# Bias tables of a neighbourhood attention: assembled in DRAM ahead of time, loaded with one transfer each

## The chip, the cores and the metric

The kernel runs on one core of one Trainium2 chip. The metric is device time in microseconds of one execution, and the median of several runs is compared. The core has five engines with a queue each, executed in order: TensorE (PE, with its weight loads as PEld), VectorE (DVE), ScalarE (ACT), GpSimd (POOL) and SyncE (SP). SP computes nothing; in this kernel it issues nearly all DMA transfers. Sixteen DMA engines carry them out. PEclk is the clock that the throttle granted to PE, as a share of full speed.

## The reference

One layer of a diffusion backbone over 1024 latent tokens (a grid of 16 rows by 64 columns) and 256 context tokens, model width 1024: a modulated RMSNorm, one input projection to attention heads and to a Hyena long-convolution group, both groups side by side, an output projection, and a SwiGLU feed-forward part. What the change touches is the learned bias of the neighbourhood attention. There are 8 heads of 64; each query sees a window of 8 rows by 16 columns and all context keys, in one softmax:

```python
dr = row_idx - r[:, None] + (WIN_ROWS - 1)
dc = jnp.clip(col[None, :] - col[:, None], -(WIN_COLS - 1), WIN_COLS - 1) + (WIN_COLS - 1)
bias = rpb[:, dr[:, None, :, None], dc[None, :, None, :]].astype(jnp.float32)
s_loc = jnp.einsum('bhrqd,bhrikd->bhrqik', qg, k_band).astype(jnp.float32) * scale
s_loc = jnp.where(col_in[None, None, None, :, None, :], s_loc + bias[None], NEG)
...
p = jax.nn.softmax(jnp.concatenate([s_loc, s_ctx], axis=-1), axis=-1).astype(v.dtype)
```

`rpb` has 15 row offsets by 31 column offsets for each head; `NEG` is -1e30, so that places outside the window weigh nothing.

## The kernel before

A planner puts the instructions of each engine in order: it takes the program's order as priority, estimates when each can start, and inserts the semaphores. A tile with one buffer (`bufs=1`) passes from one user to the next in program order, and the next user waits until the former is done with it. What an engine's queue holds is fixed at build time; if an instruction's input is late, everything behind it on that engine waits too.

The stages that matter, with their times in the profile:

- **Projection** (to about 606 us). A loop over j = 0 to 3 and `which` = 0 to 2 calls `qkv(j, which)` and `hy_chunk(which, j)`. Each calls `proj`, which loads 128 columns of weights (L606, tile `wr`), splits them into a high and a low part and does 72 matmuls per 128 columns (L116 to L118) into three PSUM banks of tag `p`. A `sink` evicts the banks: `qkv` to a tile `cv0` or `cv1`, `hyin` likewise with a width-3 convolution (L638 to L646). These two `cv` tiles take turns. `hy_chunk` then makes sums and differences in the tile `fo` (L663 to L667, one buffer), transposes them and stores them to `lxd` and `cxd`. Pieces of the modulation (`adaln`, tile `wada` with one buffer, L221 and L225) are put between.
- **Filters.** Inside the first turn, `filters` builds the spectra of the Hyena filters, with PE work of its own (L376, and L116 to L118 into banks `fA` and `fB`). The planner mixes it with the projection until about 420 us.
- **Bias frames.** After the turn j = 0, `rpb_frames` runs for three variants (`var`: left edge, middle, right edge of the grid). Each fills a tile with `NEG` on POOL, places the 16 windows of columns with 16 small loads (L556), reorders it (L557) and stores it to the DRAM tensor `rpw` as variant x query column x head x 4 x 120 (L558). These frames use the tile `fo`.
- **Chains.** `chain(j)`, j = 0 to 4, does the long convolution by matmuls with DFT tables and twiddles, on PE (L802, L872), DVE (L816 to L860), POOL (L823 to L885) and ACT; it loads `s` (L788) and `K` (L837) on SP and stores `hyd`. Chains have a raised priority; they start beside the projection and go on beside the attention.
- **Attention** (606 to about 917 us). `attend(p_)` works on a pair of heads. It loads q, k and v (L1004 to L1010) and the bias tables `tbs[h][var]`: six tiles of 128 x 736 f32, one per head of the pair and variant, with one buffer each. A table holds 128 queries (8 rows by 16 columns), for the upper and the lower half of the grid side by side (11 and 12 key rows by 32 columns). All of it outside the windows is `NEG`, filled once by POOL before the loop (L941). `bias_load` writes the rest: for each of 16 query rows one copy (L959) from `rpw`, because the window moves with the row. That makes 16 copies a table of 64 pieces of 256 B, 96 a pair, 384 in all. `scores` multiplies q by k (L1021), and one DVE instruction (L1042) adds the table to the scores and takes the row maximum; exponentials on ACT (L1055, L1056), transposes (L1065), the product with v (L979) and the normalisation (L1111) follow.
- **Output projection and feed-forward** (after 917 us): not touched.

Of the kernel before, what the change touches and what calls it, by code (L numbers as in the profile page):

```python
# [11 lines left out]
F32 = mybir.dt.float32  # L12
# [7 lines left out]
P = 128  # L20
# [3 lines left out]
LT = LL + LC  # L24
NH, DH = 8, 64
# [4 lines left out]
NEG = -1e30  # L30
# [44 lines left out]
HALF_ROWS = ((0, 11), (4, 12))  # L75
# [11 lines left out]
def _build(nc, tc, top, V, A, G, T, Q, I, O, dbg, upto):  # L87
# [458 lines left out]
    NROW = HALF_ROWS[0][1] + HALF_ROWS[1][1]  # L546
    HOFF = (0, HALF_ROWS[0][1] * 32)
    rpw = dr.tile([3, 16, NH, 4, 120], F32, name="rpw")

    def rpb_frames(t, var):  # L550
        f, g = t[:, 0:480], t[:, 512:992]
        G.memset(f, NEG)
        fv = f.rearrange("p (r c) -> p r c", c=32)
        for cq in range(16):
            a = (8 + max(cq - 8, 0), cq, min(cq, 8))[var]
            Q.dma_start(out=fv[cq * 8:cq * 8 + 8, :, a:a + 16], in_=I["rpb"][0][:, :, a + 7 - cq:a + 23 - cq])  # L556
        G.tensor_copy(g.rearrange("p (u r c) -> p r u c", u=4, r=15), f.rearrange("p (r u c) -> p r u c", u=4, r=15))  # L557
        Q.dma_start(out=rpw[var].rearrange("q h u x -> (q h) (u x)"), in_=g)  # L558
# [93 lines left out]
    def hy_chunk(which, j):  # L652

        cv = hyin((8, 0, 4)[which] + j)
        v = cv[:, 0:LL].rearrange("p (j r) -> p r j", r=4)
        lo, up = v[:, :, 0:128], v[:, :, 255:127:-1]
        clo, cup = cv[:, LL:LL + 128], cv[:, LL + 255:LL + 127:-1]
        fo = ip.tile([P, 2, 640], F32, tag="fo", name="fo", bufs=1)
        for i in range(2):
            d, dc = fo[:, i, 0:512].rearrange("p (r j) -> p r j", r=4), fo[:, i, 512:640]  # L660
            if which < 2:
                f = G.tensor_sub if i else G.tensor_add
                f(d, up, lo)  # L663
                f(dc, cup, clo)
            else:
                A.copy(d, up if i else lo)
                V.tensor_copy(dc, cup if i else clo)  # L667
        for i in range(2):
            ps = bk("tB")
            for r in range(4):  # L670
                T.transpose(ps[:, r * P:(r + 1) * P], fo[:, i, r * P:(r + 1) * P], ident)
            t = ip.tile([P, 512], F32, tag="st", name="st", bufs=2)
            A.copy(t, ps)
            Q.dma_start(out=lxd[j, which, :, i], in_=t)
        ps = bk("tB")
        for i in range(2):
            T.transpose(ps[:, i * P:(i + 1) * P], fo[:, i, 512:640], ident)
        t = ip.tile([P, 2, P], F32, tag="st", name="cx", bufs=2)
        A.copy(t, ps[:, 0:256].rearrange("p (i c) -> p i c", i=2))
        Q.dma_start(out=cxd[which, :, :, j * P:(j + 1) * P], in_=t)  # L680

    def qkv(p_, which):


        w_ = 16 if which == 0 else 8
        t = ip.tile([P, LT], F32, tag=f"cv{turn_('cv')}", name="qkv", bufs=1)

        def sink(ps, c0, n):
            if c0 < LL:
                r0 = c0 // GW  # L690
                src = ps.rearrange("p (r u c) -> p r u c", r=n // GW, c=w_)
                A.copy(t[:, 0:LL].rearrange("p (u r c) -> p r u c", r=16, c=w_)[:, r0:r0 + n // GW], src)
            else:
                A.copy(t[:, LL:LT], ps)

        proj(win[:, :, which * 512 + p_ * P:which * 512 + (p_ + 1) * P], sink, DH ** -0.5 if which == 0 else 1.0)
        if which < 2:
            Q.dma_start(out=(qd, kd)[which][p_, :, 0:LT], in_=t)
        if which == 0:
            return  # L700
        ctx = t[:, LL:LT]
        ps = bk("tB")
        for i in range(2):
            T.transpose(ps[:, i * P:(i + 1) * P], ctx[:, i * P:(i + 1) * P], ident)
        pv = ps[:, 0:256].rearrange("p (n c) -> p n c", n=2)
        so = ip.tile([P, 2, P], F32, tag="st", name="so", bufs=2)
        A.copy(so, pv)
        for i in range(2):
            Q.dma_start(out=O[1 + which][0, 0, 2 * p_:2 * p_ + 2, i * P:(i + 1) * P].rearrange("h t d -> t h d"),
                        in_=so[:, i].rearrange("p (h d) -> p h d", h=2))  # L710
        if which == 2:
            vstore(so, 8, 2, p_)
            for g in range(2):
                ps = bk("tB")
                for i in range(4):
                    T.transpose(ps[:, i * P:(i + 1) * P], t[:, (4 * g + i) * P:(4 * g + i + 1) * P], ident)
                vt = ip.tile([P, 4, P], F32, tag="st", name="vt", bufs=2)
                A.copy(vt, ps.rearrange("p (n c) -> p n c", n=4))
                vstore(vt, 4 * g, 4, p_)
# [17 lines left out]
    for j in range(4):  # L737
        for which in range(3):
            if j + which > 0:
                qkv(j, which)  # L740
            hy_chunk(which, j)
            if j + which == 0:

                t = ft([P, 512], "tm", bufs=2)
                e = "p a b -> p (a b)"
                Q.dma_start(out=t, in_=I["t_dft"].flatten().rearrange("(p x) -> p x", p=P))
                split(t, dft[0].rearrange(e), dft[1].rearrange(e))
                Q.dma_start(out=dlt, in_=I["t_delta"])
                Q.dma_start(out=nt, in_=I["t_nt"])
                with tc.issue_after(wloads[-1]):  # L750
                    Ws0 = w3load(0)
                filters(hs1, hs2, Ws0)
        cached(j)
        if j == 0:
            for var in range(3):
                rpb_frames(ip.tile([P, LT], F32, tag="fo", name="rp", bufs=1), var)
    fes.close()
    fbk.close()
    cbk = Banks("bkc", "right", "tile", cA=(1, 3))
# [176 lines left out]
        V.memset(t, 0.0)  # L936

    tbs = [[tp.tile([P, NROW * 32], F32, name=f"tb{h}{v}") for v in range(3)] for h in range(2)]
    for t in tbs:
        for v in t:  # L940
            G.memset(v, NEG)  # L941

    BLK = ((1, 4), (0, 4), (0, 4), (0, 3))
    Pring = [[tp.tile([P, 2, b - a, 16, 8], F32, name=f"Pl{h}{i}") for i, (a, b) in enumerate(BLK)] for h in range(2)]
    for r in Pring:
        for t in r:
            G.memset(t[:, 0, :, 11:16], 0.0)
            G.memset(t[:, 1, :, 0:4], 0.0)
    def bias_load(h, var):

        t = tbs[h % 2][var]
        for half in range(2):
            for rq in range(8):
                r = 8 * half + rq
                r0 = min(max(r - 4, 0), 8)
                nr = HALF_ROWS[half][1]
                a, d = r0 - HALF_ROWS[half][0], r0 - r + 7
                tv = t[rq * 16:(rq + 1) * 16, HOFF[half]:HOFF[half] + nr * 32].rearrange("q (u x) -> q u x", u=4)
                Q.dma_start(out=tv[:, :, a * 8:a * 8 + 64], in_=rpw[var, :, h, :, d * 8:d * 8 + 64])  # L959

    def stat(name, n=2):
        return tp.tile([P, n], F32, tag=name, name=name, bufs=4)

# [37 lines left out]
    def attend(p_):  # L1001
# [9 lines left out]
                        in_=I["cache_ctx_v"][0, 0, 2 * p_ + h].rearrange("(n p) d -> p n d", p=P))  # L1011
        for var in range(3):
            for h in range(2):
                bias_load(2 * p_ + h, var)
        kg = k[:, 0:LL].rearrange("p (u x) -> p u x", u=8)
        hs = [slice(h * DH, (h + 1) * DH) for h in range(2)]
        Pc = {}
# [747 lines left out]
```

## Time and profile before

| | us |
|---|---|
| three runs: lowest, median, highest | 1920.3, 1921.23, 1921.35 |
| the profiled execution: its time | 1918.35 |
| its span, from first to last instruction | 1916.6 |

Over the span PE is busy 1748.7 us (91%), DVE 1372.6 us (72%), ACT 885.0 us (46%) and POOL 412.4 us (22%); the mean granted clock of PE is 0.947. These are averages over stages that differ much: in the first slices of the feed-forward part all of PE's time is taken, while in the slices of the attention it is 0.7 to 0.9. So what follows is read by stretches of time, one row a stretch: start and end, its length, the busy time of PE, PEld, DVE, ACT and POOL, each with its number of instructions, then the granted clock, the share of the 16 DMA engines that was busy, and GB/s. In rows of the timeline the first number is the start, the second the duration; brackets hold the idle time before it and what ended it. A row of waits reads: who waited for whom, us in total, times, the longest one. A row of an instruction group in a tile's view has the shortest, median and longest duration in ns.

The transfer counts by kind show how much SP has to issue for the tables: `tb<-rpw` x384 of 16.0 KB each; the next most frequent kinds are `wada<-in_w_ada_dram` and `rp<-in_rpb_dram` with x48 each.

### The profile page before, as it was taken

What the parts mean: (1) busy time and instruction counts of PE and PEld (TensorE: products, weight loads), DVE (VectorE), ACT (ScalarE), POOL (GpSimd) and SP (SyncE); (2) the same over time, 40 slices, a digit from 0 to 9 for tenths busy, and PEclk for the clock granted to TensorE, in tenths of its full rate; (3) what the DMA queues carried; (4) which work ended last, traced back from release to release, by engine and by line L of the source; (5) the groups of instructions that cost most, each with busy time, mean ns of one, the idle gap of its engine ahead of it and who ended that gap; (6) DMA issues with size and microseconds to landing.
All of it is one profiled execution on the core that took longest, in us unless ns stands there. A gap on an engine that the chain in (4) does not pass through costs nothing.

```text
span 1916.6 us, 27816 instructions
## 1 busy us (share of the span) xinstructions
PE 1748.7 (91%) x9999; PEld 1468.5 (77%) x9999; DVE 1372.6 (72%) x2175; ACT 885.0 (46%) x1827; POOL 412.4 (22%) x331
## 2 busy tenths in 40 slices
PE   5899989999994789789899699999999999999998
PEld 1688877887773345445688599999999999788786
DVE  4667648747777776776455888888877777656887
ACT  4654435434333355455555544444444444443352
POOL 2354546543654322233100000000000000000001
PEclk7999989999997799799899799999999999999999
DMA  7424444455433334421622154555322222853663
GB/s 266 133 75 129 130 128 119 143 170 170 139 111 122 84 96 94 108 63 56 209 99 100 57 161 163 164 168 173 114 72 73 72 62 71 286 184 109 207 209 127
DMA packets 238267, 249.80 MB, mean 130 GB/s; under 512 B 56610, under 2 KB 187795, under 8 KB 237873
## 3 DMA queue, kind: packets, MB, share of 16 engines
q1 hardware_dynamic: 236168, 247.09, 41.2%
q8 instruction: 79, 1.29, 0.3%
q10 hardware_dynamic: 1705, 0.82, 0.2%
q14 instruction: 59, 0.48, 0.1%
q0 software_dynamic: 256, 0.11, 0.0%
HBM read 176.75 MB, written 71.20 MB: 129 GB/s over the span
## 4 chain that ended last, share of the span: by engine, by line
PE 36%; DVE 10%; DMA 6%; issue 3%; ACT 3%; POOL 1%; SPq 0%; DVEq 0%; POOLq 0%; ACTq 0%
PE psd L118 6%; PE psd L116 6%; PE psd L117 6%; PE psa L116 2%; PE psa L117 2%; PE psa L118 2%; DMA wt<-in_w_down_dram 2%; DMA tdr<-wt 2%; PE psc L117 1%; PE psc L118 1%; PE psc L116 1%; PE psb L117 1%; PE psb L118 1%; PE psb L116 1%; DVE cv L1514 1%
## 5 line engine op out<-in xcount | busy, mean ns | idle before, releaser
L116 PE MATMUL psp<-hh,wh 128*128 128x512 f32 (+1 forms) x552 | 203.1, 368 | 2.3 <-ACT wh L121 1.9
L117 PE MATMUL psp<-hl,wh 128*128 128x512 f32 (+1 forms) x552 | 201.1, 364 | 0.0
L118 PE MATMUL psp<-hh,wl 128*128 128x512 f32 (+1 forms) x552 | 200.3, 363 | 0.0
L1680 POOL TENSOR_TENSOR rs<-rs,mhalf 128x1 f32<-128x1 f32 x10 | 7.7, 770 | 812.5 <-DVE rs L1679 812.5
L116 PE MATMUL psa<-T,ws 128*128 128x256 f32 (+1 forms) x528 | 166.1, 315 | 3.1 <-ACT rows L1480 3.0
L117 PE MATMUL psa<-T,ws 128*128 128x256 f32 (+1 forms) x528 | 165.6, 314 | 2.8 <-DVE T L1207 2.8
L118 PE MATMUL psa<-T,ws 128*128 128x256 f32 (+1 forms) x528 | 165.0, 313 | 0.0
L116 PE MATMUL psd<-wd,gs 128*128 128x512 f32 x360 | 140.5, 391 | 3.1 <-ACT gs L121 3.1
L117 PE MATMUL psd<-wd,gs 128*128 128x512 f32 x360 | 140.9, 391 | 0.0
L118 PE MATMUL psd<-wd,gs 128*128 128x512 f32 x360 | 124.9, 390 | 1.6 <-DVE gs L122 1.6
L116 PEld LDWEIGHTS psp<-hh,wh 128*128 128x128 f32 x552 | 106.5, 193 | 23.7 <-issue 7.0
L117 PEld LDWEIGHTS psp<-hl,wh 128*128 128x128 f32 x552 | 106.7, 193 | 15.0 <-issue 1.2
L116 PE MATMUL psc<-T,ws 128*128 128x384 f32 (+1 forms) x352 | 110.3, 313 | 8.4 <-ACT ws L121 8.4
L118 PEld LDWEIGHTS psp<-hh,wl 128*128 128x128 f32 x552 | 106.0, 192 | 14.9 <-issue 0.8
L117 PE MATMUL psc<-T,ws 128*128 128x384 f32 (+1 forms) x352 | 110.3, 313 | 0.0
L118 PE MATMUL psc<-T,ws 128*128 128x384 f32 (+1 forms) x352 | 110.1, 313 | 0.0
L117 PE MATMUL psb<-T,ws 128*128 128x384 f32 (+1 forms) x352 | 109.7, 312 | 0.0
L118 PE MATMUL psb<-T,ws 128*128 128x384 f32 (+1 forms) x352 | 109.6, 311 | 0.0
L116 PE MATMUL psb<-T,ws 128*128 128x384 f32 (+1 forms) x352 | 109.5, 311 | 0.0
L116 PEld LDWEIGHTS psa<-T,ws 128*128 128x128 f32 x528 | 101.4, 192 | 4.6 <-ACT rows L1480 4.5
L117 PEld LDWEIGHTS psa<-T,ws 128*128 128x128 f32 x528 | 101.5, 192 | 3.1 <-DVE T L1207 3.1
L118 PEld LDWEIGHTS psa<-T,ws 128*128 128x128 f32 x528 | 101.1, 192 | 0.0
(391 smaller groups left out, 4821.2 us busy)
## 6 DMA issues: line engine op xcount, KB each, us to landing
wada<-in_w_ada_dram SPq DMA_DIRECT2D x48, 512.0 KB
wr<-in_w_up_dram SPq DMA_DIRECT2D x44, 512.0 KB
gr<-gdr SPq DMA_DIRECT2D x44, 320.0 KB
wr<-in_w_in_dram SPq DMA_DIRECT2D x23, 512.0 KB
wt<-in_w_down_dram SPq DMA_DIRECT2D x44, 256.0 KB
tdr<-wt SPq DMA_DIRECT2D x44, 256.0 KB
gdr<-cv SPq DMA_DIRECT2D x22, 512.0 KB
wr<-tdr SPq DMA_DIRECT2D x20, 512.0 KB
```

The source lines that it names most:

```text
L116: T.matmul(out, ah, bh, start=start, stop=False, skip_group_check=True)
L117: T.matmul(out, ah, bl, start=False, stop=False, skip_group_check=True)
L118: T.matmul(out, al, bh, start=False, stop=stop, skip_group_check=True)
L1514: V.scalar_tensor_tensor(cv, r[:, 2:NC + 2], ffw(2, ch), cv, op0=ALU.mult, op1=ALU.add)
L1680: G.tensor_tensor(rs, rs, mhalf, op=ALU.pow)
```

## The change

The 24 tables (8 heads x 3 variants) get a place of their own in DRAM, `biasd`. After the bias frames, at the end of the turn j = 0, one more tile `fo` is filled with `NEG` and stored 24 times, once for each table. In the turns j = 1 and j = 2, `bias_rows` copies the windows from `rpw` into `biasd`, DRAM to DRAM: j = 1 the upper half of the grid, j = 2 the lower, with `which` for the variant, four query rows before `hy_chunk` and four after. One copy takes all heads of one query row and one of its four groups of columns (`u`), so there are 3 x 16 x 4 = 192 of them. In the attention the fill of the tables and `bias_load` go; `attend` loads each table with one transfer of 128 x 736 f32, 24 in all.

```diff
@@ -546,6 +546,26 @@
     rpw = dr.tile([3, 16, NH, 4, 120], F32, name="rpw")
+    biasd = dr.tile([NH, 3, P, NROW * 32], F32, name="biasd")
+
+    def bias_blank(t, h):
+
+        if h == 0:
+            G.memset(t[:, 0:NROW * 32], NEG)
+        for var in range(3):
+            Q.dma_start(out=biasd[h, var], in_=t[:, 0:NROW * 32])
+
+    def bias_rows(var, half, rqs):
+
+        for rq in rqs:
+            r = 8 * half + rq
+            r0 = min(max(r - 4, 0), 8)
+            nr = HALF_ROWS[half][1]
+            a, d = r0 - HALF_ROWS[half][0], r0 - r + 7
+            tv = biasd[:, var, rq * 16:(rq + 1) * 16, HOFF[half]:HOFF[half] + nr * 32].rearrange(
+                "h q (u x) -> u q h x", u=4)
+            for u in range(4):
+                Q.dma_start(out=tv[u, :, :, a * 8:a * 8 + 64], in_=rpw[var, :, :, u, d * 8:d * 8 + 64])
@@ -738,7 +758,11 @@
             if j + which > 0:
                 qkv(j, which)
+            if j in (1, 2):
+                bias_rows(which, j - 1, range(4))
             hy_chunk(which, j)
+            if j in (1, 2):
+                bias_rows(which, j - 1, range(4, 8))
@@ -754,6 +778,9 @@
             for var in range(3):
                 rpb_frames(ip.tile([P, LT], F32, tag="fo", name="rp", bufs=1), var)
+            t = ip.tile([P, LT], F32, tag="fo", name="rp", bufs=1)
+            for h in range(NH):
+                bias_blank(t, h)
@@ -936,9 +963,6 @@
-    for t in tbs:
-        for v in t:
-            G.memset(v, NEG)
@@ -946,18 +970,6 @@
-    def bias_load(h, var):
-
-        t = tbs[h % 2][var]
-        for half in range(2):
-            for rq in range(8):
-                r = 8 * half + rq
-                r0 = min(max(r - 4, 0), 8)
-                nr = HALF_ROWS[half][1]
-                a, d = r0 - HALF_ROWS[half][0], r0 - r + 7
-                tv = t[rq * 16:(rq + 1) * 16, HOFF[half]:HOFF[half] + nr * 32].rearrange("q (u x) -> q u x", u=4)
-                Q.dma_start(out=tv[:, :, a * 8:a * 8 + 64], in_=rpw[var, :, h, :, d * 8:d * 8 + 64])
@@ -1011,7 +1023,7 @@
         for var in range(3):
             for h in range(2):
-                bias_load(2 * p_ + h, var)
+                Q.dma_start(out=tbs[h][var], in_=biasd[2 * p_ + h, var])
```

## The prediction

> **What bounds the kernel now.** I read the page's head, then the busy time of each engine by stretches, the table tile's view, and the waits of the attention stage.
>
> ```profile
> span 1916.6 us, 27816 instructions
> core 0: us, PE busy (x) PEld busy (x) DVE busy (x) ACT busy (x) POOL busy (x), PEclk, DMA share, GB/s
> 269.00:289.00 20.00, 14.90 (x83) 13.13 (x81) 12.50 (x18) 11.82 (x31) 15.99 (x12) 0.74 0.19 54
> 300.00:420.00 120.00, 119.69 (x753) 100.91 (x746) 86.27 (x117) 55.46 (x122) 61.99 (x39) 1.00 0.46 135
> 460.00:606.00 146.00, 124.50 (x646) 99.77 (x644) 108.65 (x157) 51.25 (x123) 77.20 (x51) 0.90 0.37 117
> 606.00:618.00 12.00, 0.00 (x0) 0.00 (x0) 11.97 (x17) 0.74 (x2) 10.34 (x27) 0.50 0.75 239
> 618.00:629.00 11.00, 7.76 (x22) 4.81 (x22) 4.86 (x12) 4.21 (x12) 3.81 (x4) 0.68 0.23 35
> 629.00:677.00 48.00, 35.07 (x154) 18.70 (x154) 36.34 (x84) 22.78 (x78) 15.31 (x11) 0.75 0.45 123
> 677.00:685.00 8.00, 8.00 (x47) 4.58 (x47) 5.88 (x12) 4.68 (x18) 2.53 (x2) 1.00 0.28 47
> 685.00:732.00 47.00, 36.66 (x222) 22.07 (x220) 38.62 (x88) 24.75 (x81) 14.54 (x10) 0.93 0.38 90
> 732.00:775.00 43.00, 35.66 (x239) 22.93 (x237) 28.38 (x52) 24.30 (x74) 7.69 (x6) 0.96 0.37 89
> 775.00:837.00 62.00, 50.68 (x281) 28.96 (x279) 45.08 (x103) 32.08 (x110) 20.01 (x14) 0.86 0.36 82
> 837.00:917.00 80.00, 71.33 (x415) 44.69 (x415) 52.21 (x113) 41.46 (x123) 28.03 (x17) 0.96 0.19 62
> ```
>
> Outside the change's reach PE sets the pace: in 300 to 420 us, the middle of the input projection, it is busy 119.69 of 120 us. In the attention, 618 to 837, nothing is full: adding its six rows gives PE 173.8 and DVE 159.2 of 219 us, 79% and 73%. What is full there is SP's queue:
>
> ```profile
> L959 SPq DMA_DIRECT2D tb<-rpw x384: 302/424/1596, 612.1 to 835.6; - x192
> 612.10 16.18 SPq L959 DMA_DIRECT2D tb<-rpw  x30
> 786.86 40.90 SPq L959 DMA_DIRECT2D tb<-rpw  x80
> 629.67 0.43 DVE L1042 CUSTOM_DVE_ANT_0 Pl<-psS,tb 128x264 f32<-128x264 f32 x1 [1.94 <-PE psS L1021]
> DVE Pl L1042 <- DMA tb<-rpw: 8.9, 6, 2.5
> POOL s L828 <- DMA tb<-rpw: 16.5, 1, 16.5
> PE pscA L872 <- DVE s L860: 21.7, 5, 14.4
> SPq L837 <- DVE s L842: 5.5, 3, 3.5
> 855.15 0.42 DVE L1042 CUSTOM_DVE_ANT_0 Pl<-psS,tb 128x264 f32<-128x264 f32 x1
> ```
>
> 384 table copies are issued from 612.1 to 835.6 us, one each 0.51 to 0.54 us in the two runs shown (0.424 us for the issue itself), with almost nothing else between. So the first pair's scores, from 629.67, go at the pace of 16 issues a tile. But DVE stood still for the tables only 8.9 us in all; POOL's 16.5 us is a chain step that waited behind. The queue is full, yet it is only one of several things that are late.
>
> **The change, part by part.** Times are summed against the profiled execution's own 1918.35 us (1.75 more than its span); the median of the runs shown, 1921.23, lies 2.9 above.
>
> *Removed from the attention:* 384 issues of 0.424 us, 163 us of SP, and six fills of the tables on POOL:
>
> ```profile
> L941 POOL MEMSET tb<- x6: 708/708/708, 607.2 to 610.4; 128x736 f32 x6
> 608.29 7.85 DVE L931 COPY sel<-ident 128x64 f32<-128x64 f32 x8
> L837 SPq DMA_DIRECT2D K<-Kd x16: 320/337/430, 424.7 to 827.9; - x16
> 1660.00:1690.00 30.00, 30.00 (x134) 24.86 (x133) 16.99 (x24) 13.80 (x23) 0.00 (x0) 1.00 1.03 388
> ```
>
> The fills (6 x 0.708 = 4.2 us) cost nothing now: DVE copies `sel` until 616.1 and the chain waits for that. Without this cover they would cost their 4.2. *Added:* 24 loads of 376,832 B. As K's contiguous loads they cost 24 x 0.337 = 8 us of SP; at the 388 GB/s of the saturated stretch 1 us each, 23 us of DMA over the stage. The first two can be there some 2 us after the q, k and v loads, against 16 issues (8 us) for one table now.
>
> How much does this free? The bound from below is DVE's named wait, 9 us. The bound from above is all of 618 to 837 at the PE pace of 837 to 917, which has no table copies: PE busy 0.89 at clock 0.96. Weighted by the clock, PE's six rows hold 151.5 us at full clock; 151.5 / (0.89 x 0.96) = 177, so 42 us. I take DVE at 80%, near the 82% (38.62 of 47) that it reached in 685 to 732: 159.2 / 0.80 = 199, **-20 us**. DVE at 90% would be needed for the 42, which no row shows.
>
> What is late next is DVE together with the Hyena chains, in one another's queues (PE's 21.7 us behind DVE's L860). The loads also bring a new wait: a table of the next pair may land only when DVE has read that of this pair. Behind the waiting load on SP stand the chains' K and s loads and the next q, k, v; POOL and DVE wait for K. That is worth nothing to 10 us (K's loads on SP now wait 5.5 us for DVE); I take the planner's order as good, **+1**.
>
> *Added in the projection, first part:* one fill and 24 stores of the blank (9.04 MB), in tile `fo`, which has one buffer that the next Hyena chunk needs.
>
> ```profile
> 276.94 0.34 SPq L558 DMA_DIRECT2D rpw<-rp  x1
> 235.54 0.48 DVE L646 SCALAR_TENSOR_TENSOR cv<-psp,vec,cv 128x255 f32<-128x255 f32 x1
> 280.83 2.13 POOL L663 TENSOR_TENSOR fo<-cv 128x512 f32<-128x512 f32 x1
> 288.58 1.88 ACT L638 ACTIVATE cv<-psp,vec 128x512 f32<-128x512 f32 x3
> L118 PE MATMUL psp<-hh,wl 128*128 128x256 f32 x2 | 0.6, 282 | 0.0
> L116 PE MATMUL psp<-hh,wh 128*128 128x512 f32 (+1 forms) x136 | 48.9, 360 | 0.0
> L118 PE MATMUL psp<-hh,wl 128*128 128x512 f32 (+1 forms) x135 | 47.8, 354 | 0.0
> L116 PE MATMUL psfA<-csh,dft 128*128 128x256 f32 x64 | 18.4, 287 | 0.2 <-DVE GO L420 0.2
> 261.56 0.44 SPq L489 DMA_DIRECT2D Kc<-GO  x1
> 261.00:266.00 5.00, 5.00 (x24) 4.14 (x23) 0.00 (x0) 1.04 (x1) 2.11 (x1) 1.00 0.86 313
> ```
>
> These rows show a stall that is already there. The chunk's `cv` was finished at 235.54 us, but `fo` belonged to the third bias frame until 276.94 (and its landing), so the sums began at 280.83. Only then did a `cv` come free, and at 288.58 ACT evicted three banks in one go that PE had long filled. From 269 to 289 PE did two projection matmuls of this form (0.6 us); the filters filled 14.9 us at clock 0.74, 11.0 us at full clock.
>
> The blank stands between frame and chunk, so it prolongs this very stall: fill 0.7 us, then 9.04 MB at between 313 GB/s (the 1 MB store at 261.56) and 388, 23 to 29 us, and a landing: 28 us. In 28 us PE loses 28 x (1 - 11.0/20) = 13 us, if the filter work done meanwhile is saved later, or 28 x 0.7 = 20 if it isn't: in 300 to 420 the projection's three forms (first and last shown) were busy some 49 us each, the filters' three, of which the first is shown, some 18, so about 0.7 of PE's time is the projection's. I take 14. From 300 to 420 PE is full, so all of it is carried on; in 460 to 606 PE is idle for 21.5 us, and a third of that should take up 7: **+7**, within 0 and 20.
>
> *Second part:* 192 copies DRAM to DRAM, each 16 x 8 pieces of 256 B, together as many pieces (24,576) as the copies removed. Before has no copy of this kind; the nearest rows:
>
> ```profile
> L467 SPq DMA_DIRECT2D Kd<-GO x32: 359/462/523, 143.4 to 401.6; - x32
> L556 SPq DMA_DIRECT2D rp<-in_rpb_dram x48: 653/667/1402, 200.1 to 272.5; - x48
> 792.00:827.00 35.00, 30.49 (x179) 18.52 (x175) 24.48 (x62) 22.34 (x79) 6.68 (x4) 0.95 0.23 35
> q1 hardware_dynamic: 5685, 1.17, 22.2%
> ```
>
> At 0.424 to 0.667 us they take 81 to 128 us of SP, between some 305 and 500 us. In 792 to 827, table copies alone, 5685 packets used 22.2% of 16 engines for 35 us: 22 ns a packet, so 24,576 take 33.6 us of all engines. In 300 to 420 alone 54% of 120 us, 65 us, is free. They are ready as soon as the blanks have landed, so the planner can lay them into SP's gaps; the weight and `wada` loads queued behind one lose half a microsecond, behind a group of 16 some 7 us, and PE waits where a `wada` load has no lead. Between 0 and 15 I take **+3**, as groups of this size now stand between the attention's loads without a long wait.
>
> The Trainium skill, "DMA: Bandwidth & Descriptors", section Specifications, speaks against this part: it wants pieces of at least 512 B, as shorter ones are written by read-modify-write. Before only reads such pieces from DRAM, so no run here shows the price; if each write doubled its packet, the copies would take 67 us of the engines.
>
> Sum: -20 + 1 + 7 + 3 = **-9**, 1909.3 in the profile, **1912 us** in the median.
>
> **The rivals.** (a) *The queue was the whole cause:* the attention gains near its upper bound, -38, and the projection pays 8: -30, 1891. For it speaks SP's full queue; against it that DVE's work alone needs 159 of the 219 us, and its wait for tables is 8.9. (b) *The tables were in time:* only the 9 us named go, and the projection gives them back (+10): 1922. For it: the fourth pair's scores begin at 855.15, when its last table copy had long been issued (835.6). (c) *Slower:* the held `fo`. It decides where what the projection really loses exceeds the attention's gain: with 20 us lost and nothing taken up, the row copies at 5 and a gain of 12, +13, 1934. For it speaks the stall at 269 to 289, which has the same cause; against it the idle 21.5 us later. (d) *Short writes to DRAM cost double:* twice 33.6 us of all engines no longer pass beside the projection's loads, and SP's issues at 0.667 us crowd the weights; +20 on the sum, 1932. The rule of the Trainium skill quoted above would be its reason. (e) *It doesn't do what it says:* each row copy waits for the one before, so that the tables are late. A landing took about 2 us (276.94 to 280.83, with POOL busy between); 192 in a row are some 400 us, and the attention would start late, 1945. Against it: Kd's interleaved stores are issued 0.46 us apart.
>
> **How the numbers follow.** Forecast 42%, (a) 20%, (b) 13%, (c) 17%, (d) 5%, (e) 3%. The forecast's own range is 1902 to 1922. The range of 8 in 10 is 1887 to 1936: it holds (a) but for its far end, (b) and most of (c). A change of 0.2%, 3.8 us, is about the least that a measurement tells from none: faster 0.56 (most of the forecast, all of (a)), same 0.15 (most of (b) and an edge of the forecast), slower 0.29.
>
> **What would show it.** SP's table loads shrink to 24 rows and the first score comes before 625 us after the same start; DVE's share in the attention rises towards 80%. In the projection `fo` of the next chunk starts some 28 us later than the last frame's store, with PE on filters alone; if it doesn't, the +7 falls. Row copies near 0.45 us each, with PE waits for `wada` still small, would bear out the +3. The prediction is wrong if the attention stays over 300 us with the tables early, or if the stage before it ends over 20 us later.

## The result, and the profile after

The changed kernel takes **1965.22 us** (median of 4 runs, 1962.99 to 1971.18) against 1921.29 us before (4 runs, 1920.3 to 1922.8): a ratio of **1.0233**, 95% interval 1.0209 to 1.0257. It is 44 us slower. The forecast was 9 us faster, and 1965 lies above the range (1887 to 1936). The profiled execution is the one of 1962.99 us.

First, where the time appeared. These rows are the first and last matmuls of the attention, from the views of its score banks and of its probability-times-v banks. Behind each group stand the shortest, median and longest duration in ns, and then the starts of the first and the last instruction in us. First before, then after:

```profile
L1021 PE MATMUL psS<-k,q x288: 376/480/1007, 628.9 to 886.2; 64*128 64x256 f32 x81, 64*128 64x288 f32 x16, 64*128 64x352 f32 x16, 64*128 64x384 f32 x16
L979 PE MATMUL psav<-pt,vs x384: 379/379/690, 646.2 to 913.0; 128*64 128x256 f32 x192
```

```profile
L1033 PE MATMUL psS<-k,q x288: 376/456/1006, 682.1 to 924.2; 64*128 64x256 f32 x80, 64*128 64x264 f32 x16, 64*128 64x288 f32 x16, 64*128 64x352 f32 x16
L991 PE MATMUL psav<-pt,vs x384: 379/379/634, 699.0 to 953.6; 128*64 128x256 f32 x192
```

The first score starts at 682.1 instead of 628.9 us: everything ahead of the attention became 53.2 us longer. From first score to last matmul the attention takes 271.5 instead of 284.1 us, 12.6 less. Together that is 40.6 us; the spans differ by 44.6 (1961.2 against 1916.6), so 4 more come after the attention. The change does what it says in the attention. It loses four times as much in the projection.

What it says shows in the view of the table copies of the changed kernel: 24 loads stand where 384 stood, 0.346 us of SP each, behind 24 blank stores and (quoted below) 192 row copies.

```profile
L1026 SPq DMA_DIRECT2D tb<-biasd x24: 319/346/1453, 663.5 to 854.0; - x24
L556 SPq DMA_DIRECT2D biasd<-rp x24: 333/866/1021, 281.0 to 300.6; - x24
```

Where in the projection? Busy time by stretches, before and after; the columns are the stretch, its length, the busy time of PE, PE's weight loads, DVE, ACT and POOL with their instruction counts, the granted clock, the DMA engines' share and GB/s.

```profile
269.00:340.00 71.00, 64.32 (x398) 53.73 (x397) 55.36 (x78) 38.65 (x91) 47.06 (x31) 0.93 0.37 107
400.00:450.00 50.00, 50.00 (x296) 41.57 (x295) 19.61 (x35) 18.62 (x44) 13.91 (x9) 1.00 0.68 214
400.00:500.00 100.00, 96.40 (x545) 79.37 (x544) 57.16 (x94) 37.23 (x85) 37.51 (x24) 0.98 0.55 171
```

```profile
269.00:340.00 71.00, 53.90 (x287) 47.25 (x286) 49.39 (x73) 34.09 (x84) 41.59 (x31) 0.78 0.60 197
400.00:450.00 50.00, 17.91 (x103) 12.03 (x102) 6.20 (x14) 6.57 (x17) 7.72 (x6) 0.63 0.65 191
450.00:500.00 50.00, 50.00 (x277) 41.21 (x277) 6.58 (x12) 12.66 (x20) 12.25 (x7) 1.00 0.62 169
400.00:500.00 100.00, 67.91 (x379) 53.25 (x378) 12.79 (x26) 19.23 (x37) 19.98 (x13) 0.81 0.64 180
```

Three things can be seen. From 269 to 340 us PE loses 10.4 us: this is where the forecast put the `fo` tile held by the blanks (e8 below tests it). From 400 to 450 PE is busy for 17.9 of 50 us: a hole for which no step of the prediction has a price. And DVE does 12.8 us of work from 400 to 500 instead of 57.2: even where PE is full again (450 to 500), DVE has almost nothing to do.

What stood in SP's queue at that time? Its timeline, with the start, the time taken, the line and the count of each run of equal issues:

```profile
307.35 10.51 SPq L568 DMA_DIRECT2D biasd<-rpw  x16
317.95 0.54 SPq L694 DMA_DIRECT2D lxd<-st  x1
...
436.17 0.52 SPq L568 DMA_DIRECT2D biasd<-rpw  x1
436.78 0.53 SPq L694 DMA_DIRECT2D lxd<-st  x1
437.36 0.43 SPq L626 DMA_DIRECT2D wr<-in_w_in_dram  x1
```

From 307 us on SP issues row copies and what lies between them. The weight load (`wr`) at 437.36 is the 14th of the projection's 23; before, the 14th was issued at 323.9. Counted over the whole timeline from 307 us, exactly 128 row copies stand ahead of it. That is the 96 of the loop's step `j` = 1 and the first 32 of step 2: all copies that come before this load **in the program**. Thirteen weight loads (5 of step 0, 6 of step 1 and two of step 2) had gone out by 272 us, long ahead of their use, when the copies couldn't start yet because the blanks weren't written. So the first load that had not yet gone met the copies of all the steps that were prefetched already. The rows of the tiles, first after, then before (the dftf rows are the load of the Hyena chain's DFT table and the chain's first matmuls, which read it):

```profile
L568 SPq DMA_DIRECT2D biasd<-rpw x192: 510/597/1952, 307.3 to 489.9; - x192
L626 SPq DMA_DIRECT2D wr<-in_w_in_dram x7: 379/535/612, 437.4 to 498.8; - x7
L791 SPq DMA_DIRECT2D dftf<-in_t_dft_dram x1: 1117/1117/1117, 493.4 to 493.4; - x1
L829 PE MATMUL pscA<-s,dftf x32: 377/379/380, 500.9 to 555.5; 128*128 128x256 f32 x32
```

```profile
L606 SPq DMA_DIRECT2D wr<-in_w_in_dram x9: 377/384/872, 323.9 to 484.7; - x9
L764 SPq DMA_DIRECT2D dftf<-in_t_dft_dram x1: 2096/2096/2096, 426.7 to 426.7; - x1
L802 PE MATMUL pscA<-s,dftf x48: 377/379/483, 436.6 to 541.2; 128*128 128x256 f32 x48
```

The second late transfer is `dftf`: 493.4 instead of 426.7 us, and the chain's first matmul follows at 500.9 instead of 436.6. That is why DVE is idle: from 437 us on the chain was its work.

What PE itself waited for in its hole stands in its waits from 300 to 600 us in the changed kernel:

```profile
PE pstB L225 <- DMA wada<-in_w_ada_dram: 17.7, 3, 11.2
PE pstB L752 <- DMA ck<-in_cache_ctx_k_dram: 8.4, 1, 8.4
PE psp L116 <- ACT wh L121: 7.8, 1, 7.8
```

The last of them is `wh`, the high part split from the 14th weight load; it ends the hole at 444.4 us. Ahead of it, from 405 us on, PE waited for a load of the context cache (`ck`) and for two loads of the modulation (`wada`), which stood behind row copies as well. None of these three waits is in the same view of the kernel before. So the prediction's warning of a `wada` load without a lead came true too; the 14th weight load is the one of these late loads that came last.

The theory to test (**Q**) is that the copies' time on SP makes ready transfers late, by their place in an in-order queue. Its rivals: the held `fo` (**B**), the transfers themselves, DRAM to DRAM in pieces of 256 bytes (**D**), and SP's summed time whatever stands behind what (**S**).

### The profile page after: what moved, and what is told of

Read it like the earlier page. It is cut to its first block, busy times and chain, and to the rows that moved or that the text cites. A ratio compares the mean times of both kernels' runs of the same rounds, so it can differ in the third digit from the quotient of the medians.

```text
span 1961.2 us, 27556 instructions
## 1 busy us (share of the span) xinstructions
PE 1746.4 (89%) x9999; PEld 1468.0 (75%) x9999; DVE 1364.3 (70%) x2175; ACT 885.3 (45%) x1827; POOL 402.1 (21%) x326
## 4 chain that ended last, share of the span: by engine, by line
PE 38%; DVE 7%; DMA 4%; issue 2%; ACT 2%; POOL 1%; SPq 0%; POOLq 0%; DVEq 0%; ACTq 0%
PE psd L118 6%; PE psd L116 6%; PE psd L117 6%; PE psa L116 3%; PE psa L117 3%; PE psa L118 3%; PE psc L117 2%; PE psc L118 2%; PE psc L116 2%; PE psb L117 2%; PE psb L118 2%; PE psb L116 2%; DMA wt<-in_w_down_dram 1%; DMA tdr<-wt 1%; DVE T L1219 1%
```

## The experiments

All ratios are to the kernel before, run on the same chip in the same series, with the 95% interval. "14th load" is the issue of the first weight load after 300 us, "dftf" that of the table, "score" the start of the first score matmul, all in us from the profile of that kernel. The median of the kernel before was 1921.29 us in the series of the changed kernel and 1916.40 to 1917.37 us in those of the experiments, so kernels of different series are compared by their ratios.

| kernel | us | ratio | 14th load | dftf | score |
|---|---|---|---|---|---|
| before | 1921.29 | 1 | 323.9 | 426.7 | 628.9 |
| changed | 1965.22 | 1.0233 (1.0209–1.0257) | 437.4 | 493.4 | 682.1 |
| e1 no row copies | 1921.94 | 1.0019 (1.0007–1.0032) | 349.3 | 417.3 | 640.6 |
| e2 copies from GpSimd | 1999.55 | 1.0428 (1.0409–1.0447) | 350.4 | 465.3 | 705.2 |
| e3 copies from ScalarE | 1949.08 | 1.0158 (1.0142–1.0174) | 406.1 | 425.0 | 679.4 |
| e4 behind own weight load | 1957.54 | 1.0205 (1.0181–1.0229) | 440.7 | 495.1 | 684.9 |
| e5 behind the loop | 1948.27 | 1.0178 (1.0149–1.0207) | 348.4 | 504.8 | 673.6 |
| e6 64 merged copies | 1908.90 | 0.9956 (0.9941–0.9971) | 373.9 | 420.8 | 631.0 |
| e7 before, no table loads | 1909.01 | 0.9966 (0.9952–0.9980) | 326.1 | 428.7 | 631.7 |
| e8 e1, blanks by DRAM | 1902.44 | 0.9925 (0.9899–0.9951) | 321.5 | 431.4 | 625.0 |
| e9 e6, blanks by DRAM | 1923.69 | 1.0028 (1.0014–1.0043) | 387.6 | 439.2 | 643.0 |
| e10 e6, copies twice | 1973.55 | 1.0282 (1.0262–1.0302) | 440.7 | 442.0 | 684.6 |
| e11 changed, blanks by DRAM | 1965.00 | 1.0247 (1.0232–1.0262) | 447.9 | 502.6 | 692.0 |
| e12 e9, tables of one pair | 1927.15 | 1.0050 (1.0030–1.0070) | 388.8 | 436.5 | 639.6 |
| e13 192 copies behind dftf | 1918.73 | 1.0011 (0.9997–1.0026) | 349.7 | 427.6 | 639.0 |
| e14 64 copies behind dftf | 1907.50 | 0.9949 (0.9933–0.9965) | 348.1 | 420.6 | 630.0 |
| e15 e14, blanks by DRAM | 1897.00 | 0.9909 (0.9879–0.9939) | 323.0 | 435.5 | 627.4 |

### Is it the row copies or the blanks? (e1, e11, e8)

e1 takes both calls of the row copies out of the loop:

```diff
-            if j in (1, 2):
-                bias_rows(which, j - 1, range(4))
             hy_chunk(which, j)
-            if j in (1, 2):
-                bias_rows(which, j - 1, range(4, 8))
```

> The 192 row copies are left out (so the local scores get a table that is blank everywhere); the 24 blank stores, the fo tile that they hold and the attention's six whole tables per pair stay. Theory Q, the row copies are the loss (they fill SP's queue from 307 to 490 us, and ready weight loads wait behind them): the projection gives back some 40 us of the 51 that it grew by, the weight load that came at 437 us comes before 350 us, and the time is 1915 to 1930 us. Rival B, the blank stores holding fo are the loss: the projection keeps at least 30 us of its growth and the time stays at 1945 to 1965 us.

1921.94 us, a ratio of 1.0019 instead of 1.0233: 41 of the 44 us are gone, so the row copies are the loss, and B falls as its main cause. PE is full from 400 to 450 again (50.00 of 50 us), and DVE does 61.55 us of work from 400 to 500:

```profile
400.00:500.00 100.00, 94.73 (x535) 77.22 (x534) 61.55 (x87) 35.64 (x81) 42.36 (x28) 0.98 0.46 147
269.00:340.00 71.00, 54.91 (x307) 47.07 (x307) 50.72 (x75) 32.61 (x80) 41.51 (x31) 0.78 0.58 198
```

From 269 to 340 us PE still has 9.4 us less than before (54.91 against 64.32). That is the blanks' part. e8 and e11 hold `fo` for one store only and copy that table in DRAM, with (e11) and without (e8) the row copies:

```diff
-            Q.dma_start(out=biasd[h, var], in_=t[:, 0:NROW * 32])
+            Q.dma_start(out=biasd[h, var], in_=biasd[0, 0] if h + var else t[:, 0:NROW * 32])
```

> As e1 (row copies left out), but only the first blank table is stored from the fo tile, and the other 23 are copied from that one in DRAM, so that fo is held for some 5 us instead of 28; the bytes written stay. If the held fo is what the blank stores cost, some 8 us come back against e1 in the stretch 269 to 340 us and the time is 1908 to 1916 us. Rival W: the 9 MB of writes crowd the DMA engines (full from 289 to 300 us), whatever they are read from, and the time stays at 1918 to 1926 us.

> The changed kernel with all its 192 row copies; only the blank tables go by DRAM (one store from the fo tile, 23 copies of it), so that fo is held for some 5 us instead of 28. By the held fo as a cost of its own: 8 to 20 us less than the changed kernel, 1945 to 1957 us. If fo's hold is covered by the longer lateness that the row copies make: 1960 to 1968 us. It can't be under 1935 us if the row copies are the larger cost.

e8 takes 1902.44 us (0.9925 against e1's 1.0019, 18 us), which is 6 us under its range:

```profile
269.00:340.00 71.00, 63.36 (x381) 55.08 (x380) 45.68 (x73) 34.54 (x80) 38.60 (x27) 0.90 0.64 199
```

Its PE is busy for 63.36 us from 269 to 340, nearly as before (64.32), with the same bytes written, and the sums in `fo` start at 287.83 instead of e1's 310.07 us: rival W falls, the held `fo` was the cost. The busy time alone, 8.5 us more than in e1, understates it. Weighted by the granted clock (0.90 and 0.78), as the prediction weighted it, it is an estimated 14 us more, and the first score comes 15.6 us earlier. In e11, with the 192 copies in place, the same edit gives back nothing (1965.00 us):

```profile
269.00:340.00 71.00, 62.46 (x369) 53.34 (x368) 48.40 (x71) 35.59 (x83) 42.29 (x29) 0.93 0.61 186
400.00:450.00 50.00, 14.69 (x97) 9.02 (x95) 5.67 (x13) 6.53 (x16) 5.30 (x5) 0.59 0.63 189
```

PE wins 8.6 us early (62.46 against 53.90) and then stands still for longer in 400 to 450, because the 14th load comes at 447.9 all the same. A cost that lies ahead of a larger wait is hidden by it.

### Another queue? (e2, e3)

```diff
-                Q.dma_start(out=tv[u, ...], in_=rpw[var, ...])
+                G.dma_start(out=tv[u, ...], in_=rpw[var, ...])
```

(`A` in e3.)

> The same 192 row copies with the same bytes, but GpSimd's queue issues them instead of SP's. Theory Q, the place in SP's queue is the loss: the weight loads are no longer behind them, the projection loses at most 15 of its 51 us of growth to them, and the time is 1920 to 1935 us (GpSimd also makes the fo tiles, so a little may stay). Rival D, the transfers themselves are the loss (DRAM to DRAM in pieces of 256 bytes, which crowd the weights on the DMA engines): nothing is won and the time stays at 1955 to 1970 us.

> The same 192 row copies, issued from ScalarE's queue. Theory Q: the weight loads on SP are free of them, but ScalarE itself makes the split weights and empties PSUM, and each copy takes it about 0.6 us of issue, 115 us in all in a stage where it is the partner of TensorE; so part of the loss comes back: 1930 to 1955 us. Rival D: 1955 to 1970 us, as in the changed kernel.

e2 is the clearest miss: 1999.55 us, outside both ranges and worse than the changed kernel. But D isn't borne out by it either, since it expected no change. GpSimd pays for its issues in busy time. POOL's busy time from 300 to 540 us, in the changed kernel and then in e2, e2's copies, and a wait of its PE (us in all, times, longest):

```profile
300.00:540.00 240.00, 86.75 (x56) 0.88 0.57 158
```

```profile
300.00:540.00 240.00, 176.30 (x247) 0.84 0.50 149
```

```profile
L568 POOL DMA_DIRECT2D biasd<-rpw x192: 528/528/629, 307.1 to 537.8; - x192
```

```profile
PE psp L118 <- POOL wl L122: 13.3, 1, 13.3
```

192 issues of 0.528 us are 101 us of an engine that also makes the projection's split weights (`wl`) and `fo`; PE waits 13.3 us for one `wl` (its longest wait there; for `wada` it waits 20.8 us in seven). The loss moved with the copies to another queue with work of its own in it. e3 ends at 1949.08 us, inside theory Q's range: before it empties banks ScalarE waits for its own copies, 46 us in these rows.

```profile
ACT qkv L712 <- DMA biasd<-rpw: 13.4, 4, 6.9
ACT tm L417 <- DMA biasd<-rpw: 12.5, 2, 10.0
ACT cv L658 <- DMA biasd<-rpw: 10.8, 3, 5.2
ACT kt L754 <- DMA biasd<-rpw: 9.2, 1, 9.2
```

### Another place on SP? (e4, e5)

e4 keeps the 32 copies of each turn of `which` behind that turn's own weight load; e5 puts all 192 behind the loop.

```diff
+                with tc.issue_after(wloads[-1]):
+                    bias_rows(which, j - 1, range(8))
```

```diff
     for j in range(4):
 ...
+    for half in range(2):
+        for var in range(3):
+            bias_rows(var, half, range(8))
     fes.close()
```

> The same row copies on the same SP queue; each group of 32 is only kept behind the weight load of its own step in the queue's order. Theory Q, in the form that the order is the loss (weight loads behind some hundred copies): no weight load waits behind more than 32 copies, the hole in TensorE at 400 to 450 us goes, and the time falls to 1925 to 1945 us. Rival S, the sum of SP's issue time is the loss (192 copies of 0.6 us and their gaps, whatever stands before what): SP stays full up to 480 us or more, other transfers become late instead, and the time stays at 1950 to 1970 us. Rival D: 1955 to 1970 us.

> The same 192 row copies on SP's queue, but all behind the projection's last chunk in program order, so that no weight load stands behind one. Theory Q: the weight load that came at 437 us in the changed kernel comes before 360 us, TensorE is busy again from 400 to 450 us, and what stays is the first pair of heads waiting for its tables, since the copies fill SP for some 115 us from about 510 to 560 us on: 1930 to 1950 us. Rival D, the copies' transfers are the loss wherever they run: 1955 to 1970 us.

e4 missed theory Q's range: 1957.54 us, and the 14th load at 440.7 is as late as ever. The ranges of S and D hold this time, so e4 doesn't speak against them. Theory Q's expectation counted each load against the copies of its own turn. But this load is one of step 2, and all copies of step 1 still precede it. e5 frees it (348.4) and fills PE's hole, and yet 1948.27 us remain. DVE shows why: it is busy for 19.83 us from 400 to 500.

```profile
400.00:500.00 100.00, 94.45 (x548) 77.42 (x547) 19.83 (x39) 27.33 (x48) 22.32 (x14) 0.98 0.65 182
```

```profile
L790 SPq DMA_DIRECT2D dftf<-in_t_dft_dram x1: 1606/1606/1606, 504.8 to 504.8; - x1
L828 PE MATMUL pscA<-s,dftf x26: 377/379/634, 509.4 to 559.8; 128*128 128x256 f32 x26
```

The load of `dftf` follows the loop in the program, so all 192 copies still stand ahead of it. The chain starts at 509.4 us, and what DVE didn't do beside the projection it does later, with PE less busy: 42.04 of the 60 us from 560 to 620, in e13 (below) 55.80. The expectation named the wrong wait (the first pair's tables); the late `dftf` was found here.

### By the copy, or by the piece? (e6, e10)

e6 copies the three variants at once: 64 copies of 384 pieces, as many pieces and bytes as 192 of 128. They stand with `which` = 0 of steps 1 and 2, so all 64 still precede the 14th load in the program.

```diff
-                Q.dma_start(out=tv[u, :, :, a * 8:a * 8 + 64], in_=rpw[var, :, :, u, d * 8:d * 8 + 64])
+                Q.dma_start(out=tv[u, :, :, :, a * 8:a * 8 + 64],
+                            in_=rpw[:, :, :, u, d * 8:d * 8 + 64].rearrange("v q h x -> q h v x"))
```

> The same rows in 64 copies of 384 pieces of 256 bytes instead of 192 copies of 128 pieces (the three variants in one copy, issued with the first chunk of a group instead of with each). If SP pays by the copy, about 0.6 us each, the copies take it 38 us instead of 115, weight loads wait a third as long, and the time is 1925 to 1942 us. If it pays by the piece (128 pieces in 0.6 us: 384 in some 1.9 us), SP is full just as long, and the time stays at 1950 to 1970 us.

```profile
L568 SPq DMA_DIRECT2D biasd<-rpw x64: 528/625/1759, 308.9 to 373.3; - x64
L627 SPq DMA_DIRECT2D wr<-in_w_in_dram x8: 373/384/617, 373.9 to 484.0; - x8
```

A copy of three times the pieces takes SP 0.625 us instead of 0.597: SP pays by the copy. The 14th load comes at 373.9, right behind the last of them, and the kernel takes 1908.90 us (0.9956 against 1.0233: 53 us less), 16 us under the range of this reading. The DMA engines move the same bytes in the same pieces, so D falls for this amount of bytes. e10 issues each merged copy twice:

> e6 with each merged copy issued twice: 128 copies of 384 pieces, which move twice the bytes of the changed kernel's 192 copies, but take SP about 128 times 0.63 us, 80 us, instead of 115 us. Theory Q, SP's time per copy: between e6 and the changed kernel, 1920 to 1945 us. Rival D, pieces of 256 bytes on the DMA engines: as slow as the changed kernel or slower, 1960 to 2000 us.

```profile
L569 SPq DMA_DIRECT2D biasd<-rpw x128: 528/620/1679, 307.7 to 446.0; - x128
L628 SPq DMA_DIRECT2D wr<-in_w_in_dram x6: 380/385/617, 440.7 to 499.2; - x6
```

```profile
400.00:450.00 50.00, 25.10 (x149) 20.01 (x148) 7.99 (x18) 10.22 (x22) 9.05 (x7) 0.74 0.94 255
```

1973.55 us: theory Q's number was missed, and D's range holds it. Q's own rule was misapplied, since in this kernel all 128 copies precede the 14th load in the program, as in the changed one, and it comes at 440.7 against 437.4. From the first copy to this load the queue took, per copy ahead of the load, (437.4 - 307.3) / 128 = 1.02 us in the changed kernel, (440.7 - 307.7) / 127 = 1.05 here and (373.9 - 308.9) / 64 = 1.02 in e6. That is the queue's pace with the other transfers between the copies, not the price of a copy; without copies (e1) the load comes at 349.3. So Q explains this run afterwards; the doubled bytes (DMA engines at 0.94 in that stretch) may have their part, and e10 alone doesn't tell the two apart. Here `dftf` is hardly late (442.0) and DVE does 46.01 us of work from 400 to 500; so, as far as the bytes allow the reading, the late loads of the projection are enough for the whole loss.

### Both transfers freed (e13, e14, e15)

e13 is e5 with the copies placed two lines later, behind the loads of `dftf` and `idft`; e14 is that with the merged copies, e15 also with the blanks by way of DRAM.

> As e5 (all 192 row copies on SP, behind the projection's last chunk in program order), but also behind the two loads of the Hyena chain's tables, dftf and idft. If the late weight load and the late dftf are the loss, both are free now: the chain's first matmul comes before 450 us instead of at 509, VectorE is busy over 45 of the 100 us from 400 to 500 again (e5: 20), and the time is 1908 to 1928 us. If 192 copies on SP cost their time whatever stands behind them, it stays at 1938 to 1955 us, as e5.

> e6's 64 merged copies at e13's place. By the theory of the two late transfers the weight loads come still earlier than in e6 (374 us), and the time is 1900 to 1912 us. If e6 had already lost nothing to the copies, it is within 4 us of e6's 1909 us.

> e14 with the blank tables by way of DRAM, as in e8. In e9 the weight load came at 388 us, 14 us later than in e6, and e9 was 15 us slower. If that load was e9's loss, it is gone here and the time is near e8's, 1896 to 1908 us. If the blanks by way of DRAM cost by themselves as soon as rows are copied, it is 1915 us or more.

```profile
L568 SPq DMA_DIRECT2D biasd<-rpw x192: 510/597/1783, 309.4 to 506.3; - x192
L626 SPq DMA_DIRECT2D wr<-in_w_in_dram x8: 385/535/750, 349.7 to 493.8; - x8
L828 PE MATMUL pscA<-s,dftf x48: 377/379/484, 436.5 to 538.3; 128*128 128x256 f32 x48
```

```profile
400.00:500.00 100.00, 94.97 (x540) 77.44 (x539) 54.33 (x91) 36.75 (x85) 41.68 (x27) 0.98 0.68 192
```

This settles where the loss lies. e13 has all 192 copies on SP, each as dear as in the changed kernel, from 309 to 506 us, and takes 1918.73 us (1.0011 against 1.0233): 43 us less. Only their place in the queue is different. Against e5 they have moved behind nothing but the loads of `dftf` and `idft`, which is worth 32 us by the ratios; freeing the loads of the loop (e5 against the changed kernel) brought 11. These two parts don't add up like prices, as either late transfer alone keeps the time high (e5, and with twice the bytes e10). The chain starts at 436.5 and DVE works for 54.33 us from 400 to 500. S falls as the main cause as well. A rest of it may stay: e14, with a third of the copies at the same place, is 12 us faster than e13 by the ratios, and whether SP's time or another order does that isn't shown. e14 (1907.50) and e15 (1897.00) came out as expected, but both readings given for e14 hold, as it is within 2 us of e6; **e15 beats both kernels**, 0.9% under before (0.9909, 0.9879 to 0.9939, four runs).

### What the attention can win (e7, e12)

e7 is the kernel before with its table loads left out, e9 has e6's merged copies and e8's blanks, and e12 is e9 with the table loads of three pairs of heads left out:

```diff
-        for var in range(3):
-            for h in range(2):
-                bias_load(2 * p_ + h, var)
```

```diff
+                if p_ == 0:
                     Q.dma_start(out=tbs[h][var], in_=biasd[2 * p_ + h, var])
```

> The kernel before, without its table loads in the attention at all (384 transfers left out; every local score gets the blank table, so the position bias is missing). It is the most that any better way of loading the tables can bring. By the prediction's step the attention runs 20 us shorter or more: 1885 to 1900 us. Rival V: the loads were hidden, VectorE's and the chain's own steps set the end, and the time is 1910 to 1920 us.

> The merged row copies of e6 (64 instead of 192) and the blank tables of e8 (one stored from the fo tile, 23 copied from it in DRAM) together, nothing left out. If the two costs are separate, e6's 1909 us loses up to the 20 us that the blanks gave back between e1 and e8: 1889 to 1902 us. If e8's gain needs the row copies to be absent (the copies would wait in SP's queue for blanks that are now made later and more slowly), it stays at 1904 to 1916 us.

> e9, but only the first pair of heads loads its six tables, and the other three pairs use these (their bias is that of the first two heads). So no table load waits on SP for the last reading of the table before it, with K, s, q, k and v loads behind it. If that new wait (78 us of waiting on SP in the changed kernel's attention) is a cost, 8 us or more come back against e9. If SP has room while it waits, e12 is within 4 us of e9.

e7 takes 1909.01 us (0.9966): without any table load the kernel is some 7 us faster, which is 1 us under rival V's range and 9 above the other. From first score to last matmul its attention takes 274.9 us (631.7 to 906.6), 9.2 less than before. The loads were nearly hidden. That this is the most that any better loading can bring, as the expectation says, isn't borne out: e15 loads its tables and is faster. e12 differs from e9 by 3.5 us, the wrong way: the new wait on SP costs nothing that shows beside the differences of some 10 us below. e9 itself missed: 1923.69 us. Its copies start 8 us later than e6's and the 14th load comes 14 us later (387.6), and PE is busy for 48.47 of the 60 us from 340 to 400 where e6 has 58.37; e15 moves the copies away and the loss is gone. In that stretch the waits of e9's PE name the filters' steps (10.2 us) and no load, so the way from the copies to the loss isn't shown for e9. **What stays open:** from first score to last matmul the attention of e9 takes 283.1 us and that of e12 287.0, but that of e6 271.7 and that of e15 269.7, with the same work (or, in e12, less). And e1, which has no copies, takes longer than e6, which has 64. Each edit gives another order on the engines, and differences of some 10 us that come with it are not explained here.

## Why the prediction was wrong, point by point

- **The row copies, +3 (0 to 15): this step failed.** The sentence was that the planner can lay them into SP's gaps, and that loads behind one lose half a microsecond, behind a group of 16 some 7 us. The price of an issue was right (0.424 to 0.667 us forecast, 0.597 measured), and so was SP's time (81 to 128 us forecast, 192 x 0.597 = 115). Their place was wrong. They don't stand in groups of 16 ahead of a load: 128 of them stand ahead of the first weight load that hadn't been prefetched, and all 192 ahead of `dftf`. The term was 41 us (against e1) to 43 us (against e13) instead of 3. Two signs that the prediction named against itself came: PE's waits for `wada` grew to 17.7 us, and the stage before the attention ended 53 us later, where 20 was the limit.
- **The attention, -20:** the right sign, too large. It is 12.6 us shorter in the changed kernel, and between 5.7 (e14) and 14.4 us (e15) where the projection is not late. From first score to last matmul DVE rose from 72% (205.58 of 284 us) to 77% (208.06 of 271, the row below); the 80% was assumed for a shorter stretch, 618 to 837, so only the direction compares. The step from a full SP queue to a freer DVE was mis-sized: with no table loads at all (e7) the stage is 9.2 us shorter, about the 8.9 us that DVE was named as waiting for them, which the prediction had as its bound from below. What the changed kernel, e6 and e15 win beyond 9.2 isn't explained. The sign that the prediction named, a first score before 625 us after the same start, did not come: it followed the load of q by 24.8 us (657.3 to 682.1), before by 22.5 (606.4 to 628.9).
- **The new wait on SP, +1:** not contradicted. (The 5.5 us given for K's loads before hold to 837 us; to 917 us they are 27.4.) SP waits 78.3 us in the changed kernel's attention for DVE to read a table, which looks dear, but e12 takes most of that wait away and wins nothing.
- **The held `fo`, +7 (0 to 20):** the mechanism was right. The sums of the next chunk start at 306.71 instead of 280.83 us, 26 us later (28 forecast). Taking the hold away wins 18 us (e1 to e8) and 8 to 10 us (e14 to e15), inside the bounds but above the 7. In the changed kernel it wins nothing (e11), as the larger wait behind it hides it.

```profile
682.00:953.00 271.00, 221.73 (x1316) 131.65 (x1315) 208.06 (x441) 148.05 (x479) 83.99 (x55) 0.94 0.26 83
```

```profile
SPq L1026 <- DVE m L1054: 78.3, 9, 21.8
```

```profile
306.71 2.11 POOL L683 TENSOR_TENSOR fo<-cv 128x512 f32<-128x512 f32 x1 [2.75 <-DMA Kd<-GO]
```

The three views of the changed kernel are the busy time by stretches, the waits of the attention and POOL's timeline.

- **The sum:** with the copies' term at nothing the same terms give -12; e14, which has the held `fo` and no late transfer, is 9 us under before. That the two are near is partly luck: its attention is only 5.7 us shorter (20 forecast) and its first score only 1.1 us later (7 forecast).
- **The rivals:** (d) named SP's issues crowding the weights beside the price of short writes; the first half was the cause, at twice the 20 us that it was given, and the second half isn't seen. The Trainium skill, "DMA: Bandwidth & Descriptors", section Specifications, says that transfers under 512 B are done by read-modify-write. e6 and e13 write the same 24,576 pieces of 256 B without a loss, so whatever that costs the DMA engines does not reach the time here. The prediction holds that the kernel before only reads such pieces, which is wrong: its 16 stores of `so` to `out_dram` write pieces of 256 B as well. The Trainium skill, "DMA: Bandwidth & Descriptors", section Rules for kernel authors, says to coalesce many small transfers, since under 64 KB one pays mostly overhead. This case agrees for copies of 32 KB, with the reason that the overhead is SP's: 192 of them ahead of the late loads made 1965 us, 64 of 96 KB ahead of the same weight load 1909.

## What to carry to other kernels

Price an added transfer not only by its issue time but by what stands behind it in its queue: count the copies that precede, in program order, the first load that hasn't been prefetched yet, and multiply by the queue's pace (some 1.02 us here). Here SP paid by the transfer and hardly by the piece (0.625 against 0.597 us for three times the pieces), so merge small copies, and put those that are needed late behind the last load that something waits for. And a cost that lies ahead of a larger wait shows neither when it is added nor when it is removed, so test it where the larger wait is gone.

## What was not expected of the hardware

- A DRAM-to-DRAM copy costs SP 0.597 us with 128 pieces and 0.625 us with 384. The same copy of 128 pieces costs GpSimd 0.528 us of its own busy time and ScalarE's queue 0.609 us, by this row of e3:

```profile
L568 ACTq DMA_DIRECT2D biasd<-rpw x192: 517/609/1687, 309.2 to 504.4; - x192
```

- While the copies run, SP's other issues are dearer too: a weight load takes 0.535 us in the changed kernel and in e13, and 0.384 before and in e6 (medians of the rows above).
